# The order of three matmuls in each block of a split float32 product

## The chip, the core and the metric

The kernel runs on one core of one Trainium2 chip. The metric is the device time of one execution in microseconds; several executions are timed and the median is given. A profile is one more execution, recorded by the hardware profiler.

## The reference

Two layers of a decoder on one sequence of 256 tokens with 2048 channels, all in float32. Layer 0 mixes tokens by a convolution module, layer 1 by stick-breaking attention with 16 heads; each is followed by a gated feed-forward part with a causal convolution of width 3. Cut to what matters here:

```python
for i in range(DEPTH):                      # DEPTH = 2
    shift, scale, gate = ada_ln(c, mix_mod_w[i], mix_mod_b[i])
    h = rms_norm(x, mix_norm_g[i]) * (1.0 + scale) + shift
    if i % N_MIXERS == 0:
        y = conformer_conv_module(h, ...)   # products pw1 and pw2
    else:
        y = stick_breaking_mixer(h, sb_qkv_w[j], sb_o_w[j])   # products qkv and o
    x = x + gate * y
    shift, scale, gate = ada_ln(c, ffn_mod_w[i], ffn_mod_b[i])
    h = rms_norm(x, ffn_norm_g[i]) * (1.0 + scale) + shift
    x = x + gate * conv_ffn(h, ...)         # products up (2048 to 11264) and down (5632 to 2048)
return rms_norm(x, final_norm_g)
```

## The kernel before

Activations lie with channels on the 128 partitions and the 256 tokens along the row: x is 16 tiles of 128 x 256. A product takes weights in pieces of 128 x 1024, that is eight blocks of 128 x 128. A block is one output tile `nb` (128 output channels) times one input tile `kt`.

A product in three parts replaces a float32 matmul by three matmuls in the type float32r. Weights and activations are split into a high part, which is the value cast to float32r, and a low part, which is the rest. For the weights ScalarE (ACT) makes the high tile `wh` (line 244) and VectorE (DVE) the low tile `wl` (line 248); both are in rings of four buffers. For the activations there is a pair of tiles for each kt: `zh`/`zl` for pw2 (lines 378 and 379), `hh`/`hl` for up and qk, `gh`/`gl` for down, `oh`/`ol` for o. The high tile is made on ACT, the low one behind it on DVE, out of the value and the high tile. Of each block the products high times high, high times low and low times high are summed in PSUM: three matmuls, each with its own weight load, with the activation tile as the moving operand (256 columns, 258 in a product's entry). In the code `xh` and `xl` stand for the high and low activation tiles.

`gemm` walks through the blocks of a product in the order that `plan` has written. There a product starts with a head: the first few output tiles (8 in pw2, 4 elsewhere) are done side by side, kt by kt, so that each kt serves several blocks in a row; `STAGGER` puts the last few kts of a head aside. Behind the head one output tile follows the other, and each runs through all kts.

```python
    if first > 1:
        head, nbs = nbs[:first], nbs[first:]
        s = min(stagger, len(kts) // 2)
        seq += [(n, k) for k in kts[:len(kts) - s] for n in head]
        seq += [(n, k) for n in head for k in kts[len(kts) - s:]]
    return seq + [(n, k) for n in nbs for k in kts]
```

Products in order of time: pw1 (plain float32, line 664), pw2, up and down of layer 0 in two halves, qk and v of the attention in four groups of heads (v has its own three matmuls, lines 1131 to 1133), o, up and down of layer 1. Between the blocks of pw2 some matmuls of the modulation run (line 577), and on DVE reductions for later modulations (line 331).

The order of instructions on each engine comes from the tile scheduler, which works with the program's order, dependencies and priorities; from line `in_order(here)` a stretch ahead of pw2 is fixed. Weights come over SP's DMA queue in program order, modulation rows over SP's and POOL's.

Of the kernel before, what the change touches and what calls it, by code (L numbers as in the profile page):

```python
# [117 lines left out]
def hybrid_trunk(ctx: ExitStack, tc: tile.TileContext, cfg: Cfg, io: dict):  # L118
    nc = tc.nc
# [15 lines left out]
    def psum_acc():  # L135
        return acc.tile([P, 512], F32, name="ps")
# [44 lines left out]
    def advance(gens, k):  # L181
        for g in list(gens[:k]):
            if next(g, "end") == "end":
                gens.remove(g)
# [69 lines left out]
    def pieces(name):  # L254

        for i in range(-(-len(cfg.plans[name]) // PB)):
            at = look["at"]
            assert stream[at] == (name, i)
            look["at"] += 1
            while len(raws) < min(len(stream), at + 1 + look["load"]):  # L260
                load_next()
            while len(parts) < min(len(stream), at + 1 + look["split"]):
                split_next()
            yield parts[at]

    def set_rate(name):
        for stem, rate in RATES.items():
            if name.startswith(stem):
                pace["rate"], pace["credit"] = rate

    def gemm(name, xh, xl, done, after=None, width=None, halves=0, ready=None, quiet=0,
             banks=()):

        set_rate(name)
        left, ps, paired, banks = {}, {}, [], list(banks)
        todo = -(-len(cfg.plans[name]) // PB)
        for nb, _ in cfg.plans[name]:  # L280
            left[nb] = left.get(nb, 0) + 1
        for blocks, wh, wl in pieces(name):
            for b, (nb, kt) in enumerate(blocks):
                while ready and not ready(kt):
                    advance(side, pace["heads"])
                first = nb not in ps
                if first and len(ps) < halves:
                    first = not paired
                    bank = psum_acc() if first else paired.pop()
                    ps[nb] = bank[:, 0:T] if first else bank[:, T:2 * T]  # L290
                    if first:
                        paired.append(bank)
                elif first:
                    ps[nb] = (banks.pop(0) if banks else psum_acc)()[:, :width or T]
                o = ps[nb]
                left[nb] -= 1
                c = slice(b * P, (b + 1) * P)
                nc.tensor.matmul(o, wh[:, c], xh[kt], start=first, stop=False, skip_group_check=halves > 0)  # L298
                nc.tensor.matmul(o, wh[:, c], xl[kt], start=False, stop=False, skip_group_check=halves > 0)  # L299
                nc.tensor.matmul(o, wl[:, c], xh[kt], start=False, stop=left[nb] == 0, skip_group_check=halves > 0)  # L300
                if left[nb] == 0:
                    with tc.high_priority(offset=PRIORITY):
                        done(nb, ps[nb])
            todo -= 1
            if todo < quiet:
                pace["rate"] = 0.0
            (after or tick)()
# [124 lines left out]
    class Entry:  # L432
# [31 lines left out]
        def product(self, name, done, table=None):  # L464
            need(self.m, 0)
            self.shift()
            n, state = len(cfg.plans[name]), {"i": 0}

            def after():
                state["i"] += 1  # L470
                i = state["i"]
                if i >= max(1, min(2, n // PB - 1)) and self.rs is None:
                    self.rs = self.rms.rstd()
                    if table:
                        act_tables(table)
                if self.rs is not None:
                    free = KD if i * PB >= n else min(i * PB // FIRST, max(0, KD - STAGGER))
                    with tc.high_priority(offset=PRIORITY if i * PB >= n else 0):
                        for kt in range(len(self.h), free):
                            self.h[kt] = modulate_tile(self.m, kt, self.rs, pool=kt % 8 < 5)  # L480
                tick()

            def scaled(nb, ps):
                b = tmp.tile([P, 2], F32, name="bcol", bufs=4)
                t = t256()
                nc.vector.tensor_copy(b, ps[:, T:T + 2])
                nc.vector.tensor_tensor(t, ps[:, :T], self.rs, op=ALU.mult)
                nc.scalar.activation(t, t, AF.Identity, bias=b[:, 0:1])
                done(nb, t)

            gemm(name, [self.raw[k][0] for k in range(KD)], [self.raw[k][1] for k in range(KD)], scaled, after=after,
                 width=T + 2)
            return [self.h[k][0] for k in range(KD)], [self.h[k][1] for k in range(KD)]


    with ExitStack() as cv:
# [448 lines left out]

        act_tables("sqrt_and_others")
        gemm("pw2", [z[0] for z in zs], [z[1] for z in zs], pw2_done, halves=8)
        drain(fill)


    def ffn(i, entry, out):
        m = f"ffn{i}"
        NG = KF // 2 + 1
        with ExitStack() as fs:
# [40 lines left out]

            hh, hl = entry.product(f"up{i}0a", up_done, "silu_and_others")
            gemm(f"up{i}0b", hh, hl, up_done, banks=[psum_b, psum_a])
            gemm(f"up{i}1a", hh, hl, up_done)
            need(m, 2)
# [306 lines left out]
```

## Time and profile before

| | |
|---|---|
| time, median of 3 runs | 2307.48 us (2307.41 to 2308.37) |
| profiled execution: span from its first to its last instruction | 2304.7 us; the page gives no other time of it |
| TensorE (PE) busy | 2270.8 us, 99% |
| weight loads (PEld) busy | 2168.1 us, 94% |
| DVE, ACT, POOL busy | 1736.7, 1164.4, 334.6 us |
| mean granted clock of TensorE | 0.997 |
| matmuls in the profile | 17834 |
| L298, L299 and L300 on `hh`/`hl`, `gh`/`gl` | 3264 and 1408 blocks |

Matmuls overlap: one lasts some 280 ns, and the next starts after some 117 ns. Busy time therefore says that PE always had a matmul in hand, not how fast they followed each other. To see that, one takes a stretch of the trace in which PE is busy without a break and divides its length by the number of matmuls that started in it.

The stages used below, in microseconds from the start: pw2 from 285 to 408, up of layer 0 to 668, down's first half to 792, up's second half to 1027, down's second half to 1155, attention to 1455, o to 1548, layer 1's feed-forward part to the end.

### The profile page before, as it was taken

The numbers are of one execution on the slowest core, as the hardware profiler recorded it, in microseconds if no ns is written. First come the engines' busy times: TensorE is split into PE (matmuls) and PEld (weight loads), VectorE is DVE, ScalarE is ACT, GpSimd is POOL, SyncE is SP. The second block draws the span as 40 slices with busy tenths as digits, with TensorE's granted clock in tenths as the row PEclk, the third lists the DMA queues.
The fourth block names the chain that finished last, engine by engine and source line by source line (L and its number), as shares of the span: only waits on it lengthen the run. The fifth ranks groups of instructions, "written<-read, shape, count | busy, mean of one in ns | idle before, by whom it ended". The sixth has DMA issues, their size and how long they took to land.

```text
span 2304.7 us, 44243 instructions
## 1 busy us (share of the span) xinstructions
PE 2270.8 (99%) x17834; PEld 2168.1 (94%) x17834; DVE 1736.7 (75%) x2386; ACT 1164.4 (51%) x1776; POOL 334.6 (15%) x478
## 2 busy tenths in 40 slices
PE   7999999999999999999999999999999999999997
PEld 5888678999999999999999999999999999999997
DVE  7689968899998899999975555668666545666654
ACT  2056655755543355554465555657555434555443
POOL 4058713200000000002111000121000000000010
PEclk9999999999999999999999999999999999999999
DMA  9988799789999999999854555555555555555553
GB/s 397 417 328 306 272 368 355 272 320 356 358 347 384 363 345 361 355 350 345 304 189 159 165 173 167 172 190 179 190 187 189 187 188 186 190 189 187 190 185 110
DMA packets 139167, 603.56 MB, mean 262 GB/s; under 512 B 15441, under 2 KB 15569, under 8 KB 115153
## 3 DMA queue, kind: packets, MB, share of 16 engines
q1 hardware_dynamic: 120242, 464.42, 56.0%
q0 software_dynamic: 18720, 136.32, 15.8%
q8 instruction: 139, 2.28, 0.4%
q14 instruction: 66, 0.54, 0.1%
HBM read 598.58 MB, written 2.10 MB: 261 GB/s over the span
## 4 chain that ended last, share of the span: by engine, by line
PE 88%; DVE 5%; DMA 4%; ACT 1%; issue 1%; POOL 0%; DVEq 0%; SPq 0%; POOLq 0%; ACTq 0%
PE ps L298 25%; PE ps L299 25%; PE ps L300 25%; PE ps L664 5%; DMA mraw<-in_mt_mix 3%; DVE mraw L331 2%; DVE wl L248 1%; PE ps L1133 1%; PE ps L1131 1%; PE ps L1132 1%; DMA mraw<-in_mt_ffn 1%; PE ps L577 1%; PE auxa L577 1%; DVE hl L382 0%; PE auxb L1132 0%
## 5 line engine op out<-in xcount | busy, mean ns | idle before, releaser
L248 DVE TENSOR_TENSOR wl<-raw,wh 128x1024 fp32r<-128x1024 f32 x688 | 842.9, 1229 | 412.7 <-ACT wh L244 408.0
L244 ACT CAST wh<-raw 128x1024 fp32r<-128x1024 f32 x688 | 719.5, 1048 | 823.9 <-PE ps L299 642.1
L298 PE MATMUL ps<-hh,wh 128*128 128x256 f32 (+1 forms) x3264 | 915.8, 281 | 0.0
L299 PE MATMUL ps<-hl,wh 128*128 128x256 f32 (+1 forms) x3264 | 912.1, 279 | 0.0
L300 PE MATMUL ps<-hh,wl 128*128 128x256 f32 (+1 forms) x3264 | 908.3, 278 | 0.1
L299 PEld LDWEIGHTS ps<-hl,wh 128*128 128x128 f32 x3264 | 617.7, 189 | 0.3
L300 PEld LDWEIGHTS ps<-hh,wl 128*128 128x128 f32 x3264 | 612.8, 188 | 0.7 <-DVE wl L248 0.7
L298 PEld LDWEIGHTS ps<-hh,wh 128*128 128x128 f32 x3264 | 612.7, 188 | 0.3
L299 PE MATMUL ps<-gl,wh 128*128 128x256 f32 x1408 | 396.0, 281 | 0.0
L300 PE MATMUL ps<-gh,wl 128*128 128x256 f32 x1408 | 393.7, 280 | 2.1 <-DVE wl L248 2.1
L298 PE MATMUL ps<-gh,wh 128*128 128x256 f32 x1408 | 394.9, 280 | 0.0
L331 DVE CUSTOM_DVE_ANT_0 mraw<-mraw,csr 128x2048 f32<-128x2048 f32 x152 | 348.2, 2292 | 46.3 <-DMA mraw<-in_mt_mix 30.2
L300 PEld LDWEIGHTS ps<-gh,wl 128*128 128x128 f32 x1408 | 265.5, 189 | 2.3 <-DVE wl L248 2.3
L299 PEld LDWEIGHTS ps<-gl,wh 128*128 128x128 f32 x1408 | 266.5, 189 | 0.0
L298 PEld LDWEIGHTS ps<-gh,wh 128*128 128x128 f32 x1408 | 265.6, 189 | 0.0
L397 POOL TENSOR_TENSOR sumsq<-sumsq,t 128x256 f32<-128x256 f32 x56 | 66.2, 1183 | 879.8 <-ACT t L393 879.5
L664 PE MATMUL ps<-hh,raw 128*128 128x256 f32 x832 | 188.8, 382 | 0.0
L664 PEld LDWEIGHTS ps<-hh,raw 128*128 128x128 f32 x832 | 157.8, 191 | 28.3 <-issue 5.8
L967 DVE SCALAR_TENSOR_TENSOR t<-ps,par,t 128x254 f32<-128x254 f32 x328 | 157.3, 480 | 3.9
L704 DVE SCALAR_TENSOR_TENSOR auxb<-u,cpar,auxb 128x256 f32<-128x256 f32 x297 | 121.6, 483 | 4.5 <-ACT auxb L688 3.7
L839 POOL TENSOR_TENSOR y<-y,hl 128x256 f32<-128x256 f32 x143 | 104.4, 730 | 13.4 <-ACT hl L713 3.3
L964 ACT ACTIVATE t<-ps,par 128x256 f32<-128x256 f32 x164 | 91.9, 560 | 0.0
(247 smaller groups left out, 2270.5 us busy)
## 6 DMA issues: line engine op xcount, KB each, us to landing
raw<-in_w_down SPq DMA_DIRECT2D x176, 512.0 KB, 4.5
mraw<-in_mt_ffn POOLq DMA_DIRECT2D x64, 1024.0 KB, 8.3
raw<-in_w_pw SPq DMA_DIRECT2D x96, 512.0 KB, 8.0
mraw<-in_mt_mix POOLq DMA_DIRECT2D x48, 1024.0 KB, 8.2
raw<-in_w_up01b SPq DMA_DIRECT2D x84, 512.0 KB, 7.0
raw<-in_w_up11b SPq DMA_DIRECT2D x84, 512.0 KB, 3.5
raw<-in_w_up00b SPq DMA_DIRECT2D x80, 512.0 KB, 7.6
raw<-in_w_up10b SPq DMA_DIRECT2D x80, 512.0 KB, 3.5
```

The lines of the kernel that those rows point to most:

```text
L244: nc.scalar.copy(wh[:, :n], v[:, :n])
L248: nc.vector.tensor_tensor(wl[:, :n], v[:, :n], wh[:, :n].bitcast(F32), op=ALU.subtract)
L298: nc.tensor.matmul(o, wh[:, c], xh[kt], start=first, stop=False, skip_group_check=halves > 0)
L299: nc.tensor.matmul(o, wh[:, c], xl[kt], start=False, stop=False, skip_group_check=halves > 0)
L300: nc.tensor.matmul(o, wl[:, c], xh[kt], start=False, stop=left[nb] == 0, skip_group_check=halves > 0)
L331: nc.vector.tensor_tensor_reduce(out=v, in0=v, in1=csr, scale=1.0, scalar=0.0, op0=ALU.mult, op1=ALU.add, accum_out=macc[:, nb:nb + 1])
L397: engine.tensor_tensor(self.sum, self.sum, sq, op=ALU.add)
L664: nc.tensor.matmul(banks[j][:, nb // KD * T:(nb // KD + 1) * T], w[:, b * P:(b + 1) * P], hf[kt], start=first, stop=left[j] == 0, skip_gro ...
L704: nc.vector.scalar_tensor_tensor(conv_ps[j], us[j % UBUFS][:, k:k + T], tap(j, k), conv_ps[j], op0=ALU.mult, op1=ALU.add)
L839: nc.gpsimd.tensor_tensor(ys[c], ys[c], pr, op=ALU.add)
L964: nc.scalar.activation(y, ps[:, :T], AF.Identity, bias=pc(f"fdb{i}", nb, 1), scale=w(FW - 1))
L967: nc.vector.scalar_tensor_tensor(y[:, s:], ps[:, :T - s], w(k), y[:, s:], op0=ALU.mult, op1=ALU.add)
```

## The change

The first two matmuls of each block change places: the high weights multiply the low activations first, then the high ones. The flag that starts a sum in PSUM stays with the first.

```diff
-                nc.tensor.matmul(o, wh[:, c], xh[kt], start=first, stop=False, skip_group_check=halves > 0)
-                nc.tensor.matmul(o, wh[:, c], xl[kt], start=False, stop=False, skip_group_check=halves > 0)
+                nc.tensor.matmul(o, wh[:, c], xl[kt], start=first, stop=False, skip_group_check=halves > 0)
+                nc.tensor.matmul(o, wh[:, c], xh[kt], start=False, stop=False, skip_group_check=halves > 0)
                 nc.tensor.matmul(o, wl[:, c], xh[kt], start=False, stop=left[nb] == 0, skip_group_check=halves > 0)
```

Line 298 thus reads `xl` and line 299 `xh`. Two blocks on PE behind the head of the second half of up, layer 0, kt 1 and kt 2 of one output tile, before (the names are output, moving tile, weights; the numbers behind them are buffers):

```order
L298 MATMUL ps_5556<-hh1_3805,wh_5443 128x256
L299 MATMUL ps_5556<-hl1_3806,wh_5443 128x256
L300 MATMUL ps_5556<-hh1_3805,wl_5444 128x256
L298 MATMUL ps_5556<-hh2_3812,wh_5443 128x256
L299 MATMUL ps_5556<-hl2_3813,wh_5443 128x256
L300 MATMUL ps_5556<-hh2_3812,wl_5444 128x256
```

The same two blocks on PE after:

```order
L298 MATMUL ps_5556<-hl1_3806,wh_5443 128x256
L299 MATMUL ps_5556<-hh1_3805,wh_5443 128x256
L300 MATMUL ps_5556<-hh1_3805,wl_5444 128x256
L298 MATMUL ps_5556<-hl2_3813,wh_5443 128x256
L299 MATMUL ps_5556<-hh2_3812,wh_5443 128x256
L300 MATMUL ps_5556<-hh2_3812,wl_5444 128x256
```

The weights keep their order; the high activation tile is now read by two matmuls in a row, and the next kt's low tile follows on a high one. The first two blocks of pw2 on PE before, with the semaphores that each waits for (`Activation` is ACT):

```order
L298 MATMUL ps_2395<-zh0_2259,wh_2187 128x256 [waits Activation_49,Pool_49]
L299 MATMUL ps_2395<-zl0_2260,wh_2187 128x256 [waits DVE_49]
L300 MATMUL ps_2395<-zh0_2259,wl_2188 128x256
L298 MATMUL ps_2395<-zh0_2259,wh_2187 128x256
L299 MATMUL ps_2395<-zl0_2260,wh_2187 128x256
L300 MATMUL ps_2395<-zh0_2259,wl_2188 128x256
```

The first two blocks of pw2 on PE after:

```order
L298 MATMUL ps_2395<-zl0_2260,wh_2187 128x256 [waits DVE_49,Pool_49]
L299 MATMUL ps_2395<-zh0_2259,wh_2187 128x256 [waits Activation_49]
L300 MATMUL ps_2395<-zh0_2259,wl_2188 128x256
L298 MATMUL ps_2395<-zl0_2260,wh_2187 128x256
L299 MATMUL ps_2395<-zh0_2259,wh_2187 128x256
L300 MATMUL ps_2395<-zh0_2259,wl_2188 128x256
```

The wait for DVE has moved to the first matmul. On the other engines the scheduler moves some instructions in the stage of pw2 and nowhere else. On DVE, while the z tiles are made (`y` and `t` are steps on the way to `zh`; a minus is before, a plus after):

```order
 L923 TENSOR_TENSOR y_196<-y_196,dm 128x256
 L924 TENSOR_TENSOR t<-y_196,rstd 128x256
+L248 TENSOR_TENSOR wl<-raw,wh 128x1024
 L379 TENSOR_TENSOR zl_2328<-t,zh_2327 128x256
 L923 TENSOR_TENSOR y_197<-y_197,dm 128x256
 L924 TENSOR_TENSOR t<-y_197,rstd 128x256
-L248 TENSOR_TENSOR wl<-raw,wh 128x1024
 L379 TENSOR_TENSOR zl_2336<-t,zh_2335 128x256
```

The low part of a weight piece is made ahead of the low part of kt 7 instead of behind it; two later pieces move in the same way, and their casts on ACT too.

## Prediction

> **What bounds the kernel now.** I read the page first: the busy line, the chain that ended last, and the groups of the three matmuls that the change touches.
>
> ```profile
> span 2304.7 us, 44243 instructions
> ...
> PE 2270.8 (99%) x17834; PEld 2168.1 (94%) x17834; DVE 1736.7 (75%) x2386; ACT 1164.4 (51%) x1776; POOL 334.6 (15%) x478
> ...
> L298 PE MATMUL ps<-hh,wh 128*128 128x256 f32 (+1 forms) x3264 | 915.8, 281 | 0.0
> L299 PE MATMUL ps<-hl,wh 128*128 128x256 f32 (+1 forms) x3264 | 912.1, 279 | 0.0
> L300 PE MATMUL ps<-hh,wl 128*128 128x256 f32 (+1 forms) x3264 | 908.3, 278 | 0.1
> ```
>
> PE is busy for 99% of the span, and the three lines of a block wait for nothing. Their 280 ns is the length of one matmul, which overlaps the next; what counts is the step, the time from one start to the next. The second view is the list of waits on PE: its rows from 400 us to the end (the first three here), and from the stage of pw2 (the last).
>
> ```profile
> PE ps L300 <- DVE wl L248: 2.1, 1, 2.1
> PE auxb L300 <- DVE wl L248: 0.8, 2, 0.4
> PE auxb L402 <- ACT t L393: 0.7, 1, 0.7
> PE ps L298 <- ACT t L942: 1.6, 1, 1.6
> ```
>
> So behind 400 us PE loses 3.6 us to waits, and there is nothing else to win or lose there but the step itself. The third view therefore is PE in stretches of one kind: window, busy time, matmuls, clock, DMA. Rows 1 and 2 are the up products of layer 0 behind their heads, row 3 the o product behind its head, rows 4 and 6 the heads of the two down products of layer 0, row 5 the rest of the first of them, row 7 the rest of layer 1's second.
>
> ```profile
> 442.58:668.03 225.45, 225.45 (x1934) 1.00 0.92 347
> 792.22:1027.42 235.20, 235.20 (x2019) 1.00 0.93 352
> 1477.92:1547.92 70.00, 70.00 (x603) 1.00 0.57 188
> 668.03:693.57 25.54, 25.54 (x219) 1.00 0.96 369
> 693.57:792.22 98.65, 98.65 (x843) 1.00 0.99 380
> 1027.42:1052.92 25.50, 25.50 (x218) 1.00 0.93 354
> 2193.06:2291.20 98.14, 98.14 (x839) 1.00 0.44 146
> ```
>
> The two or three matmuls that began ahead of a window are counted with it; without them these are 644, 672, 200, 72, 280, 72 and 279 blocks of three. A block takes 225.45/644 = 350.1, 235.20/672 = 350.0 and 70.00/200 = 350.0 ns in the h and o products, 98.65/280 = 352.3 and 98.14/279 = 351.8 in the rest of down, and 25.54/72 = 354.7 and 25.50/72 = 354.2 in the heads of down. Shapes, clock (1.00) and number of matmuls are the same in all, and the step differs although PE is never idle: 116.7 to 118.2 ns. The DMA share doesn't order them (0.57 gives 350.0, as 0.92 does). What distinguishes a head is in the code: four blocks in a row have the same kt, so in three of four block boundaries the high tile that ended one block (L300) is read again by the next block's first matmul. The same rise shows inside one product, on the same tiles: 354.7 - 352.3 = 2.4 and 354.2 - 351.8 = 2.4 ns.
>
> The Trainium skill ("TensorE: Matmul & The Clock Gate", section "Back-to-back issue gap") gives a step of N/2.4 + 2.5 ns at full clock, 109.2 ns for 256 columns whatever the operands, and its section "Step-by-step: what each phase is for" says that loading the next weights takes nothing from the running matmul's reads. The rows differ: at clock 1.00 no stretch is under 116.7 ns, and equal shapes differ by 1.5 ns.
>
> **The change part by part.**
>
> *Moving tiles (all 5,248 blocks; 3264 + 1408 on the page, and 576 in smaller groups).* No matmul, weight load or byte is added. The order of the weights (wh, wh, wl) stays. The moving tiles went high, low, high, then the next kt's high; they now go low, high, high, then the next kt's low. Each block thus has a low-to-high step as before, a step in which the same high tile is read twice running, and a high-to-next-low step in place of the high-to-next-high. The nearest rows for a high tile read twice running are the heads. I take their 2.4 ns per block against the rest of the same product as its price. I apply it to blocks behind heads, since the heads have that repeat already: 644 + 672 in each layer's up products (2,632), 448 in the attention's qk products behind the first (28 output tiles of 16), 200 in o: 3,280 blocks. 3,280 x 2.4 = 7.9 us. It puts them at 352.5 ns. The 1,120 blocks of down behind the heads stand at 352.05 on average without a repeat; I take them to the same 352.5, not above it, as whatever makes them slow seems to be of the same kind: 1,120 x 0.45 = 0.5 us. PE is never idle in these stretches, so all of it lies on the path. Bounds: 0 from below, if the step doesn't care; from above all blocks at the heads' 354.5: 3,280 x 4.4 + 1,120 x 2.45 = 14.4 + 2.7 = 17.1 us. A gain is bounded under the rivals.
>
> *The first matmul now waits for the low tile.* The rows of the timeline at the start of pw2:
>
> ```profile
> 285.25 0.43 DVE L379 TENSOR_TENSOR zl<-t,zh 128x256 fp32r<-128x256 f32 x1
> 285.57 0.38 PE L298 MATMUL ps<-zh,wh 128*128 128x256 f32 x1
> 285.79 0.32 PE L299 MATMUL ps<-zl,wh 128*128 128x256 f32 x1
> ```
>
> zl ends at 285.68, and the matmul that reads it began 0.11 later. The first matmul would start at 285.79 instead of 285.57: 0.2 us, on the path. The built program has 24 first reads of a low tile with a wait for DVE. The others cost at most one step each, as one matmul less stands ahead of the wait: 23 x 0.12 = 2.8 us. I take 0. In the instructions of L299 one row only shows PE idle for a low tile:
>
> ```profile
>   DVE ol L1103: 0.2, 1
> ```
>
> and in pw2, where 16 of the 24 are, the tiles lie ready long before. Here is zl of kt 7, the wl and the zl behind it, and PE's first read of kt 7:
>
> ```profile
> 311.16 0.43 DVE L379 TENSOR_TENSOR zl<-t,zh 128x256 fp32r<-128x256 f32 x1 [0.96 <-ACT zh L378]
> ...
> 312.30 1.22 DVE L248 TENSOR_TENSOR wl<-raw,wh 128x1024 fp32r<-128x1024 f32 x1
> 313.43 0.42 DVE L379 TENSOR_TENSOR zl<-t,zh 128x256 fp32r<-128x256 f32 x1
> ...
> 315.84 0.39 PE L298 MATMUL ps<-zh,wh 128*128 128x256 f32 x1
> ```
>
> *What the scheduler moves in pw2.* On DVE three wl splits now stand ahead of a zl instead of behind it, on ACT their wh casts likewise. This zl comes later by 1.22 us, or more where that wl waits for PE to give back its buffer, with the next y and zl queued behind it; the 315.84 - 311.59 = 4.2 us of lead covers it and grows further on. If that cover were gone, each of three moves could cost up to 1.2 us. Behind them a few reductions of the modulation change places with wl splits. One is this long:
>
> ```profile
> L331 DVE CUSTOM_DVE_ANT_0 mraw<-mraw,csr 128x2048 f32<-128x2048 f32 x152 | 348.2, 2292 | 46.3 <-DMA mraw<-in_mt_mix 30.2
> ```
>
> A wl behind one comes 2.3 us later, a wl ahead of one as much earlier. PE's only wait in the stage that such moves could lengthen or take away is the 1.6 us for L942. I take 0, with both ends: 1.6 us less, 2.3 us more. SP's DMAs keep their order; three of POOL's loads pass a few sums of squares and stay far ahead of their use.
>
> **Sum.** 7.9 + 0.5 + 0.2 = 8.6 us. The span of 2304.7 becomes 2313.3. The page has no other time of that execution; the median of the runs, 2307.5, lies 2.8 us over the span. Forecast: 2307.5 + 8.6 = 2316.1 us.
>
> **The rivals.**
>
> *The step doesn't care.* The counts of steps by kind stay: one low to high, one high to low, one high to high per block. If a step's length depends on these kinds, or on neither, the time is 2307.5 + 0.2 = 2307.7 us. For it: the three lines' shares of the chain are close.
>
> ```profile
> by line: PE ps L298 25.3%; PE ps L299 25.2%; PE ps L300 24.8%; PE ps L664 5.0%; DMA mraw<-in_mt_mix 3.0%; DVE mraw L331 2.0%; DVE wl L248 1.1%; issue 1.0%; PE ps L1133 1.0%; PE ps L1131 1.0%; PE ps L1132 1.0%; DMA mraw<-in_mt_ffn 0.9%; PE p
> ```
>
> Against it: the heads, which have the same kinds too, and take longer. They also change the output tile with each block, so a part of the 2.4 ns may be that and not the repeat. Chance 0.31. The skill's rule above, a step set by the columns alone, comes to the same time.
>
> *All blocks at the heads' level.* The 17.1 us above: 2307.5 + 17.1 + 0.2 = 2324.8 us. For it: every block would have a repeat, a head has one in three of four. Against: down's rest, without repeats, shows that 352 ns has other causes, which needn't add. Chance 0.14.
>
> *Reading the same tile again is cheaper: faster.* In the chain L300's matmuls have 24.8% and L298's 25.3%: 0.5% of 2304.7 = 11.5 us lie between a third of the matmuls and another. If a repeat saves as much against today's high-to-next-high step, the time is 2307.5 - 11.5 = 2296 us. It decides from 4.6 us, or 1.0 ns in each of the 4,400 blocks behind heads. Against: the heads have such repeats and are the slowest. Chance 0.12.
>
> **How the numbers follow.** Forecast 0.43 (its own range 2312 to 2321), doesn't care 0.31, heads' level 0.14, cheaper 0.12. 0.2% (4.6 us) is about what a measurement tells from no change, so: faster 0.12, same 0.31, slower 0.57. The range from 2302 to 2326 takes in the first three with pw2's ends (1.6 less, 2.3 more) and leaves out most of the last and the top of the third.
>
> **What would show it.** In the same stretches of the changed kernel: the up and o products at 352.5 ns per block (a stretch of 644 blocks in 227.0 us instead of 225.45), down's rest about the same, the heads unchanged. If the up stretches stay at 350.0, the step doesn't care; if they pass 354, the heads' level holds; under 349, a repeat is cheap. A first matmul of pw2 that starts 0.2 us later shows the moved wait. I am wrong in another way if PE shows new waits for low tiles or wl between 285 and 408 us, or if the attention's own matmuls shift.

## The result, and the profile after

The changed kernel takes 2323.0 us (median of 3 runs, 2321.1 to 2325.3) against 2307.5: slower by 0.65% (ratio 1.0065, 95% interval 1.0051 to 1.0079). The forecast was 2316.1 in a range of 2302 to 2326.

From the page of the changed kernel, the span, the busy line and the groups of the three matmuls of h (instruction, count, busy us, mean ns, idle us ahead):

```profile
span 2319.3 us, 44248 instructions
...
PE 2283.1 (98%) x17834; PEld 2179.0 (94%) x17834; DVE 1736.3 (75%) x2386; ACT 1163.3 (50%) x1776; POOL 334.3 (14%) x478
```

```profile
L300 PE MATMUL ps<-hh,wl 128*128 128x256 f32 (+1 forms) x3264 | 919.1, 282 | 0.0
L299 PE MATMUL ps<-hh,wh 128*128 128x256 f32 (+1 forms) x3264 | 915.3, 280 | 0.0
L298 PE MATMUL ps<-hl,wh 128*128 128x256 f32 (+1 forms) x3264 | 914.6, 280 | 0.0
```

The span is 14.6 us longer, PE is about as full as before, and it still waits for nothing in these lines. The names up and down take two digits from here on, the layer and the half of the product: down01 is the second half of down in layer 0; up00b is up00 without its first four output tiles, up01b is up01 without its first two. The stretches of one kind, after (window, length, busy time and matmuls, clock, DMA share, GB/s): up of layer 0 in two parts, o behind its head, the two heads of down, the rest of down00, the rest of down11.

```profile
445.72:673.27 227.55, 227.55 (x1935) 1.00 0.92 345
797.69:1035.13 237.44, 237.44 (x2018) 1.00 0.92 349
1486.92:1557.58 70.66, 70.66 (x602) 1.00 0.55 186
673.27:698.76 25.49, 25.49 (x218) 1.00 0.94 359
1035.13:1060.65 25.52, 25.52 (x219) 1.00 0.90 346
698.76:797.69 98.93, 98.93 (x842) 1.00 0.99 381
2207.32:2305.81 98.49, 98.49 (x839) 1.00 0.43 145
```

A block of up takes 227.55/644 = 353.3 and 237.44/672 = 353.3 ns instead of 350.1 and 350.0; o 70.66/200 = 353.3 instead of 350.0; the heads of down 354.0 and 354.4 (354.7 and 354.2 before); the rest of down 353.3 and 353.0 (352.3 and 351.8). By the first matmul of each stage the 14.6 us are: the four up stages 8.6 (2.06, 2.24, 2.10, 2.24), the four down stages 1.5, attention 0.6, o 0.7, pw2 2.7 and its start 0.5.

Which of the three steps grew is read from the chain of the first up stretch by line, before and then after:

```profile
by line: PE ps L298 33.3%; PE ps L299 33.2%; PE ps L300 32.8%; PE auxa L300 0.2%; PE auxa L299 0.2%; PE auxb L298 0.1%; PE auxb L299 0.1%; PE auxa L298 0.1%; PE auxb L300 0.1%
```

```profile
by line: PE ps L300 33.4%; PE ps L299 33.1%; PE ps L298 32.8%; PE auxa L299 0.2%; PE auxa L300 0.2%; PE auxb L300 0.1%; PE auxb L299 0.1%; PE auxa L298 0.1%; PE auxb L298 0.1%
```

L300 goes from 0.328 x 225.45 = 73.9 to 0.334 x 227.55 = 76.0 us, L299 from 74.9 to 75.3, L298 from 75.1 to 74.6. By the starts of the matmuls in the settled blocks of this stretch, the step from L298 to L299 went from 117.6 to 116.7 ns; the one from L299 to L300, which now leads from the first read of the high tile to the second, from 117.0 to 117.9; and the one behind L300, which now leads to the next kt's low tile, from 115.4 to 118.7. So the step between the two reads of one tile grew by 0.9 ns and the one behind them by 3.3. That is a first hint that the repeat may not be what costs, and no proof: the second read may itself fill the step behind L300.

pw2's start on PE:

```profile
286.06 0.36 PE L298 MATMUL ps<-zl,wh 128*128 128x256 f32 x1 [0.18 <-DVE zl L379]
286.25 0.28 PE L299 MATMUL ps<-zh,wh 128*128 128x256 f32 x1
```

And PE's waits (us in total, times, longest), the first in down, the other two in pw2:

```profile
PE ps L300 <- DVE wl L248: 3.3, 3, 1.9
...
PE ps L298 <- ACT t L942: 2.5, 1, 2.5
...
PE ps L298 <- DVE zl L379: 0.2, 1, 0.2
```

The moved wait is there with 0.2 us. The longer wait for `t` (2.5 for 1.6 us) comes back below.

### The profile page after: what moved, and what is told of

It is laid out like the page before. It is cut to its first block, busy times and chain, and to the rows that moved or that the text cites. A ratio compares the mean times of both kernels' runs of the same rounds, so it can differ in the third digit from the quotient of the medians.

```text
span 2319.3 us, 44248 instructions
## 1 busy us (share of the span) xinstructions
PE 2283.1 (98%) x17834; PEld 2179.0 (94%) x17834; DVE 1736.3 (75%) x2386; ACT 1163.3 (50%) x1776; POOL 334.3 (14%) x478
## 4 chain that ended last, share of the span: by engine, by line
PE 86%; DVE 6%; DMA 5%; issue 1%; ACT 1%; POOL 0%; SPq 0%; DVEq 0%; POOLq 0%; ACTq 0%
PE ps L300 25%; PE ps L298 25%; PE ps L299 24%; PE ps L664 5%; DMA mraw<-in_mt_mix 3%; DVE mraw L331 2%; DMA mraw<-in_mt_ffn 2%; DVE wl L248 1%; PE ps L1131 1%; PE ps L1132 1%; PE ps L1133 1%; PE ps L577 1%; PE auxa L577 1%; DVE hl L382 0%; PE auxb L1132 0%
## 5 line engine op out<-in xcount | busy, mean ns | idle before, releaser
L300 PE MATMUL ps<-hh,wl 128*128 128x256 f32 (+1 forms) x3264 | 919.1, 282 | 0.0
L299 PE MATMUL ps<-hh,wh 128*128 128x256 f32 (+1 forms) x3264 | 915.3, 280 | 0.0
L298 PE MATMUL ps<-hl,wh 128*128 128x256 f32 (+1 forms) x3264 | 914.6, 280 | 0.0
L298 PEld LDWEIGHTS ps<-hl,wh 128*128 128x128 f32 x3264 | 616.7, 189 | 0.3
L299 PEld LDWEIGHTS ps<-hh,wh 128*128 128x128 f32 x3264 | 613.7, 188 | 0.3
L300 PEld LDWEIGHTS ps<-hh,wl 128*128 128x128 f32 x3264 | 613.1, 188 | 0.6 <-DVE wl L248 0.6
L300 PE MATMUL ps<-gh,wl 128*128 128x256 f32 x1408 | 396.0, 281 | 3.3 <-DVE wl L248 3.3
L299 PE MATMUL ps<-gh,wh 128*128 128x256 f32 x1408 | 394.6, 280 | 0.0
L298 PE MATMUL ps<-gl,wh 128*128 128x256 f32 x1408 | 393.8, 280 | 0.0
L300 PEld LDWEIGHTS ps<-gh,wl 128*128 128x128 f32 x1408 | 264.7, 188 | 3.9 <-DVE wl L248 3.9
L298 PEld LDWEIGHTS ps<-gl,wh 128*128 128x128 f32 x1408 | 265.8, 189 | 0.0
L299 PEld LDWEIGHTS ps<-gh,wh 128*128 128x128 f32 x1408 | 264.8, 188 | 0.0
```

What stands on the lines that cost most here:

```text
L298: nc.tensor.matmul(o, wh[:, c], xl[kt], start=first, stop=False, skip_group_check=halves > 0)
L299: nc.tensor.matmul(o, wh[:, c], xh[kt], start=False, stop=False, skip_group_check=halves > 0)
```

## The experiments

Theory 1 is the prediction's: a high tile read twice running costs 2.4 to 3.3 ns, wherever it lies. Theory 2: the tiles' places decide; what it says of them changes from run to run, as each text beforehand gives it. A tile's *phase* here is its start within a partition, in units of 32 bytes, modulo 256 bytes, from the addresses in the built program. In the kernel before, hh of kt 0, 1, 2, 3 lies at phases 1, 3, 5, 7 and so on in a ring, each hl one on, and every weight slice at phase 1. The change alters the sequence of phases that PE reads: h, h+1, h becomes h+1, h, h. Where times by phase or block are given without a row, they come from the starts of the matmuls in the trace.

### Other reads in the up stages

```diff
-                matmul(wh, xh[kt]); matmul(wh, xl[kt]); matmul(wl, xh[kt])
+                up00b: (wh, xh[kt]), (wh, xh[kt]), (wl, xh[kt])
+                up01b: (wh, wh, wl) on xh[(3 * kt + 0, 1, 2) % KD]
+                up10b: (wl, xh[kt]), (wh, xh[kt]), (wh, xl[kt])
+                up11b: (wl, xh[kt]), (wh, xl[kt]), (wh, xh[kt])
```

> The kernel before, with another set of three reads in one stage each: up00b reads the high tile three times (its low products are left out), up01b reads three high tiles that follow one another in the buffer, tiles 3kt, 3kt+1, 3kt+2 modulo 16 (its low products are left out too), up10b goes wl*high, wh*high, wh*low, and up11b goes wl*high, wh*low, wh*high. All four ran at 350.1 ns a block before, and at 353.3 after the change. Theory 1, that of the prediction (a tile read twice running costs 2.4 to 3.2 ns a block, wherever it lies): up00b, with two repeats, 355 to 356.5; up01b, with none, 350; up10b, with one, 352.5 to 353.3; up11b, with none, 350. Theory 2 (a matmul's step depends on which tile follows which: from one high tile to the next high tile is the cheap step, 115.4 ns, any other takes 117.4 to 118): up00b, two repeats and one cheap step, 350 to 351.5; up01b, three cheap steps, 346 to 347; up10b, whose last step goes from low to the next high, 353; up11b, which keeps the cheap step between blocks, 350. Theory 3 (only the order of the weights counts, or nothing but the low tile's place in the block): up00b and up01b 350.

The four stretches (of the second halves, the last 580 blocks; the last 32 blocks of the first and the third row belong to up01a and up11a, which have the old reads):

```profile
442.99:671.48 228.49, 228.49 (x1934) 1.00 0.91 345
828.33:1034.23 205.90, 205.90 (x1742) 1.00 0.93 351
1589.41:1817.37 227.96, 227.96 (x1935) 1.00 0.59 191
1973.76:2176.76 203.00, 203.00 (x1743) 1.00 0.59 189
```

228.49/644 = 354.8, 205.90/580 = 355.0, 227.96/644 = 354.0, 203.00/580 = 350.0 ns. Without the 32 blocks the first and third settle at 355.0 and 354.2. The first lies in theory 1's range and the third within 0.9 ns of it, but the second doesn't: without any repeat it is as slow as the first with two. It doesn't suit theory 2 in this form either, which gave it 346. The fourth shows that the order of the weights is not it: the same sequence of moving tiles as before, with another order of weights, takes the same 350.0.

### The change everywhere but in pw2

```diff
+                x1, x2 = (xh[kt], xl[kt]) if name == "pw2" else (xl[kt], xh[kt])
```

> The change everywhere but in pw2, which keeps high, low, high. pw2 took 122.20 us from its first matmul before and 124.89 after, with 3.05 us of it in one wait on t, and started 0.49 later. If the loss in pw2 comes from its own order (its first read of zl, and the moves of the side work there), pw2 is back at 122.2 and its start at 285.6, and the span is some 3 us under that after the change: 2316.3, with the stretches of up and down as after (227.5 and 98.9 us). If it comes from what the scheduler makes of the rest, pw2 stays at 124.9 and the span at 2319.3.

The stage of pw2 as a window, and PE's waits in it (in this kernel L300 is the first matmul of a block and L944 the line that was L942):

```profile
285.89:410.30 124.41, 120.39 (x952) 1.00 0.91 350
```

```profile
PE ps L300 <- ACT t L944: 4.0, 3, 2.1
```

The span was 2316.4, as expected, but not for the reason expected: pw2 kept 124.41 us, with 4.0 us of waits for `t`, although all five engines have the order of before there. So neither branch of the expectation holds. The 2.9 us under the changed kernel lie elsewhere: 2.3 in down01 (126.3 for 128.6 us), 0.6 ahead of up.

### The order of before, other places

`SKEW` is the padding behind each high and low tile of a product, in units of 32 bytes; g0 and g1 are the tiles of down in layer 0 and layer 1.

```diff
-SKEW = {"z": (1, 1), "g0": (1, 1), "g1": (1, 1), "o": (1, 1)}
+SKEW = {"z": (1, 1), "g0": (0, 0), "g1": (1, 2), "o": (2, 2)}
-        return [hpool.tile(..., name=f"{n}{i}") for n in ("hh", "hl")]
+        return [hpool.tile(..., name=f"{n}{i}") for n in ("hl", "hh")][::-1]
```

> The order of the kernel before; only where tiles lie is changed: each pair of h is allocated low tile first, g0 has no padding, g1 has other paddings (1 and 2 for 1 and 1), o has 2 and 2. Theory 1 (the repeat alone costs, places don't): the stretches behind the heads stay where they were, h at 350.1 ns a block, down at 352.3 and 351.8, o at 350.0. Theory 2 (which tile follows which, by its place): h, where the step from high to next high keeps its distance of two slots and the other two steps change sign, moves by under 1 ns; at least one of down00 (all distances multiples of 1024 bytes) and down01 moves by more than 1 ns from 352.3 and 351.8.

The two up stretches, and down00 behind its head:

```profile
444.33:671.89 227.56, 227.56 (x1934) 1.00 0.92 344
829.73:1034.66 204.93, 204.93 (x1742) 1.00 0.93 352
697.52:797.20 99.68, 99.68 (x842) 1.00 0.98 377
```

227.56/644 = 353.4 and 204.93/580 = 353.3: the whole loss of the change, with the order of before and no tile read twice running. Only hh and hl have changed places; every engine has the instructions of the kernel before in the same order. down00, every tile at phase 5, takes 99.68/280 = 356.0. The run took 2321.3 us (one run). Theory 1's forecast for it, 350.1, falls here; so does the part of theory 2 that said h would move by under 1 ns. That a repeat costs something besides is not yet excluded. pw2, with the order and the z tiles of before, took 123.92 us in this run.

### The changed order, the same places

The edit is that of the run above, made to the changed kernel.

> The changed order, low tile first in the block, with the tiles placed as in the run with the order of before and the new places. Theory 1: as after the change, h at 353.3 ns a block, down at 353.3 and 353.0, o at 353. Theory 2 by distance: in h the step from high to the next low is now two slots on and the pair's own step one slot on, so if the cheap step is one of distance it comes back, and h is at 350 to 351; if it is one of kind (any step on to a low tile is dear, from high to next high cheap) h stays at 353.3.

Up, then down00 behind its head:

```profile
444.80:673.42 228.62, 228.62 (x1934) 1.00 0.91 343
699.05:798.73 99.68, 99.68 (x842) 1.00 0.98 376
```

None of the three: 228.62/644 = 355.0. o reached 360.0 ns, and the run took 2328.2 us, the slowest of this study (one run). So it is no rule of distance or kind; it needed a map. One thing in it speaks already: down00, where every tile is at phase 5, takes the same 99.68 us with a repeat in every block as without one in the run above.

### A map of sequences

```diff
+                if name in MAPPED and nb in MAPPED[name]:
+                    low, e, f, p = PATTERNS[MAPPED[name][nb]]
+                    h = p + f * kt        # at(x): a tile of h at phase x mod 8
+                    three = [at(h + e), at(h), at(h)] if low else [at(h), at(h + e), at(h)]
```

> A map. In the four up stages behind their heads each of 160 output tiles has its own sequence of moving tiles (so the up outputs are wrong: products are of tiles picked by address alone); all else is the kernel before. A tile's phase is its start in units of 32 bytes modulo 256. Sequence high-first: phases p, p+e, p in a block and p+f in the next; sequence low-first: p+e, p, p, and p+f in the next; e from 0 to 7, f from 1 to 7, each output tile 16 blocks. The kernel before is high-first with e=1, f=2, the changed one low-first with e=1, f=2. Theory 2, now by phase: the time of a block is a function of the sequence of phases alone, so the map repeats what other runs measured where it holds their sequence: high-first e=1, f=2 at 350.0 ns, high-first e=7, f=2 at 353.3 (the run with the low tile placed first), low-first e=1, f=2 at 353.3, low-first e=7, f=2 at 355.0; and the other sequences spread over 8 ns or more, in both orders, with the means of the two orders within 1 ns of each other. Theory 1 (a repeat costs 2.4 to 3.3 ns): high-first sequences at 350 whatever e and f, but e=0 at 355 to 357; low-first at 353.3, but e=0 at 355 to 357.

The last 8 block steps within each output tile average 348.3 to 360.0 ns over the 160 sequences; high-first means 354.4, low-first 354.6. For f=2, p=1:

```
e            0      1      2      3      4      5      6      7
high-first 355.0  353.5  353.2  355.0  353.2  351.6  350.0  355.0
low-first  355.0  353.4  351.6  355.9  355.0  355.0  355.0  354.1
```

Order as such costs 0.2 ns on average, and e=0 isn't special. Of the four known values three came again: low-first e=1 with 353.4, and from p=2, as in the runs with the low tile placed first, high-first e=7 with 353.4 and low-first e=7 with 355.0. But before's own sequence (high-first, e=1) gave 353.5, not 350.0. In the kernel before, too, the first 14 blocks of the first up stretch are uneven (350 to 360 ns) and only then repeat 348, 353, 348, 351 to the end: a sequence has to settle, and one output tile can be too short for it. (up01's stretch, which follows on down00, repeats from its first block.)

### Held phases, and longer stretches

```diff
+PATTERNS = ([(0, e, 0, p) for p in range(8) for e in range(8) for _ in range(2)] +
+            [x for x in (<eight sequences>) for _ in range(4)])
```

> A second map (the up outputs are again wrong: tiles are picked by address alone). 128 of the 160 output tiles hold the phase from block to block (p, p+e, p, for all p and e from 0 to 7, two output tiles each, so 32 blocks): in such a sequence high-first and low-first are the same sequence, turned by one. The last 32 hold eight sequences of the first map for four output tiles each (64 blocks), to see where they settle: high-first e=1 f=2 (the kernel before's own), low-first e=1 f=2 (the changed one's), low-first e=1 f=6 from p=1 and from p=2, low-first e=3 f=6, high-first e=5 f=2, high-first e=6 f=7, low-first e=6 f=6. Theory 2 by phase, with settling: the first map gave 353.5 for the kernel before's own sequence in its one output tile, since a sequence needs some 16 blocks to settle (the kernel before's first 16 blocks behind its heads ran at 353.4 and all the rest at 350.0); over 64 blocks the first settles at 350.0 in its last 32 and the second at 353.3; and the held phases, all equal in what they read, differ by 4 ns or more among themselves. If the time of a block is instead set by chance at a stage's start, the two take other values than 350.0 and 353.3. Theory 1: held phases at 350, with e=0 at 355 to 357, the same for all p.

Rows for two output tiles each (32 blocks): held e=0 at p=1, p=2 and p=7, held e=3 at p=7, and the last 32 blocks of before's sequence, of the changed one and of low-first e=6 f=6:

```profile
535.28:546.80 11.52, 11.52 (x98) 1.00 0.96 358
626.26:637.46 11.20, 11.20 (x98) 1.00 0.99 381
1772.32:1783.23 10.91, 10.91 (x98) 1.00 0.61 193
1941.34:1952.85 11.51, 11.51 (x98) 1.00 0.52 184
2009.39:2020.59 11.20, 11.20 (x98) 1.00 0.55 188
2031.91:2043.22 11.31, 11.31 (x98) 1.00 0.52 188
2167.60:2178.74 11.14, 11.14 (x98) 1.00 0.59 190
```

Before's own sequence settles at 11.20/32 = 350.0 and the changed one at 11.31/32 = 353.4, next to each other in one stage. Low-first e=6 f=6 settles at 11.14/32 = 348.1 by the row and 348.3 by its block starts: with a repeat in every block it is faster than the kernel before. One of the eight sequences, low-first e=1 f=6 from p=1, has not settled in 64 blocks (353.6, 352.5, 354.1 and 353.4 by output tile). Among held phases, e=0 (the same phase in every read) goes from 360 (p=1) over 350 (p=2) to 340 (p=7; 10.91/32 is 341 with its first blocks, and 340.0 settled). All 64, in the second output tile, over the same 8 steps as in the first map:

```
p \ e   0      1      2      3      4      5      6      7
0     355.0  353.4  360.0  353.2  351.5  353.4  356.6  353.4
1     360.0  360.0  353.2  353.5  353.4  353.2  353.4  355.6
2     350.0  353.4  353.4  353.4  355.5  353.4  355.4  353.6
3     353.4  355.0  353.4  353.4  350.2  353.2  356.6  353.5
4     360.0  356.6  352.6  356.0  356.6  355.4  353.2  353.4
5     356.1  352.9  353.4  353.2  360.0  357.9  351.5  355.9
6     351.9  353.2  356.0  353.4  355.0  355.0  354.1  353.2
7     340.0  356.6  353.2  360.0  353.4  353.4  356.8  353.4
```

p=5, e=0 is what down00 had in the two runs with other places: 356.1 here, 356.0 there, in both orders. The map carries over to another product.

### z, g and o at phase 7, in the order of before

`SHIFT` is the size of a tile, in floats, that is put ahead of the first tile of a product.

```diff
+SKEW = {"z": (0, 0), "g0": (0, 0), "g1": (0, 0), "o": (0, 0)}
+SHIFT = {"z": 32, "g0": 16, "g1": 16, "o": 16}
+        if kind not in shifted:
+            shifted[kind] = pool.tile([P, SHIFT[kind]], F32, name="shift")
```

> The order of the kernel before. Only places are changed: the tiles of z, g and o have no padding (a stride of 1024 bytes) behind a shift of 128, 64 and 64 bytes, so that every one of them starts at phase 7, the sequence that the map of held phases showed at 340.0 ns a block (and other held phases at 350 to 360). Theory 2 by phase: down behind its heads at 340.0 for 352.3 and 351.8, its heads at 340 to 342 for 354.7 and 354.2, o at 340 for 350; pw2, which waits for other engines, within 1 us of before; up unchanged. By that: 4 x (280 x 12 + 72 x 14) ns = 17.5 us and 208 x 10 ns = 2.1 us less, about 2288. If the map's figure belongs to the up stages alone (other work beside it), down stays within 350 to 356 and the time is 2303 to 2313. Theory 1: unchanged, 2307.

Up, then down00 behind its head:

```profile
444.71:670.16 225.45, 225.45 (x1934) 1.00 0.90 336
694.66:789.86 95.20, 95.20 (x843) 1.00 1.00 396
```

95.20/280 = 340.0 ns, up unchanged, 2288.2 us: ratio 0.9915 (0.9899 to 0.9932), with PE's instructions in the order of the kernel before. Two stages did not follow: pw2 took 123.7 us for 122.2, outside the expected 1 us, and down01 gained 1.3 us instead of 4.4, as PE waits there for wl (3.7 us for 2.1).

### The changed order with places for it

```diff
+            for n, i in (("hl", 1), ("hh", 0), ("hl", 0), ("hh", 3), ("hl", 3), ("hh", 2), ("hl", 2), ("hh", 1)):
+                homes_h[n, k + i] = hpool.tile([P, T + 2], F32R, name=f"{n}{k + i}")
```

> The changed order (low, high, high), with z, g and o at phase 7 as in the run beside it, and the tiles of h in other slots: high tiles at phases 2, 0, 6, 4, the low tile one on, a sequence that the second map showed settling at 351.7 with low first. Theory 2 by phase: down and o as in the run beside it, within 0.5 ns a block, though low comes first (340); up behind its heads at 351.7 for 353.3; about 2288 + 2632 x 1.7 ns + 3 us in pw2 = 2295. Theory 1: the repeat still costs 2.4 to 3.3 ns in every block, 2320 or more.

```profile
445.88:672.37 226.49, 226.49 (x1935) 1.00 0.90 336
696.86:792.06 95.20, 95.20 (x843) 1.00 1.00 396
```

Up at 226.49/644 = 351.7, down00 at 340.0 with low first as with high first. 2298.7 us, ratio 0.9962 (0.9949 to 0.9975); 3.7 us over the expected 2295. By the stages of the two profiled runs it is 4.2 us longer in up than the run beside it, as expected, and 3.4 in pw2, its start and down01 together.

### A search among the sequences that h's 32 slots allow

```diff
+                    low, *phases = PATTERNS[MAPPED[name][nb]]
+                    vh, vl = at(phases[2 * (kt % 4)]), at(phases[2 * (kt % 4) + 1])
```

> A third map (up outputs wrong, tiles picked by address alone): 80 sequences, two output tiles each, in which all eight phases serve four neighbouring k tiles, as the 32 slots of h allow; picked from all such sequences by the mean steps of tile triples in the runs so far, which give them 349.3 to 351.2 ns a block. Theory 2 by phase: settled values from 345 to 356, some under the 350.0 of the kernel before. If steps depend on the pair of tiles alone and not on how the sequence settles, all lie within 1 ns of the 349.3 to 351.2.

A miss: the 80 settle between 350.0 and 358.4, three of them at 350.0 (before's own among them, and one with low first), none under it. Mean steps of three neighbouring tiles do not foretell where a sequence settles.

### h at phase 7 too, in both orders

```diff
-        return [hpool.tile([P, T + 2], F32R, name=f"{n}{i}") for n in ("hh", "hl")]
+        return [hpool.tile([P, T + 64], F32R, name=f"{n}{i}")[:, :T + 2] for n in ("hh", "hl")]
+SHIFT = {..., "h": 48}
+        shifted["end"] = hpool.tile([P, 16], F32, name="end")
-MORE_ROWS = 4
+MORE_ROWS = 3
-                home = row_homes[n] if near else ("zmm"[n % 3] ...) if "z" in cpar else "m"
+                home = row_homes[n] if near else "m"
```

> The order of the kernel before, all moving tiles of z, g, o and now h at phase 7 (each tile of h takes 1280 bytes for 1056; for the room one of the four row buffers of the convolution and the row buffer beside z are left out, so rows of the modulation arrive later in the first 410 us), the weights at phase 1 as before. Theory 2 by phase: up behind its heads at 340.0 for 350.1 and 350.0, 26 us less than with z, g and o alone at phase 7 (2288.2), some 2 us less in attention: 2260, and 0 to 15 us back in the convolution and pw2 for the buffers: 2260 to 2275. If h doesn't follow (another pool, other neighbours), 2288 to 2303.

> The run beside it with the changed order (low, high, high) everywhere but in pw2. All tiles start at one phase, so the sequence of phases is the same in both orders. Theory 2 by phase: up, down and o at 340.0 in both, the time within 1.5 us of the run beside it: the change costs nothing where the sequence of phases does not change. Theory 1 (a tile read twice running costs 2.4 to 3.3 ns a block): 3,280 blocks and 1,120 of down, 8 to 14 us more than the run beside it.

Up, down00 behind its head and o behind its head, high first:

```profile
441.91:660.87 218.96, 218.96 (x1934) 1.00 0.92 344
685.35:780.55 95.20, 95.20 (x842) 1.00 1.01 398
1456.89:1524.89 68.00, 68.00 (x602) 1.00 0.56 193
```

The same with low first:

```profile
443.68:662.64 218.96, 218.96 (x1934) 1.00 0.91 343
687.12:782.32 95.20, 95.20 (x842) 1.00 1.01 402
1456.31:1526.98 70.67, 70.67 (x603) 1.00 0.55 186
```

High first: 2259.9 us, ratio 0.9793 (0.9781 to 0.9806), the fastest version of this study; the missing row buffers cost nothing that shows ahead of up, which began at 406.6 us (407.8 before). down01 alone gained nothing, 129.8 us for 128.0, as PE waits 6.6 us there for wl. Low first: 2264.0 us; its ratio, 0.9848 (0.9806 to 0.9889), is that of six runs, two of which took 2287.8 and 2287.9.

Up and down00 are equal to 0.01 us, 218.96/644 = 340.0 and 95.20/280 = 340.0, although every block with low first reads its high tile twice running. Theory 1 is gone there. But the medians lie 4.1 us apart and not within 1.5, and o differs, 68.00 against 70.67 us for the same 200 blocks, with the same phases in both: 340.0 and 353.3 ns. The order is not what does it. With low first too, o ran at 340.0 in the kernel of "The changed order with places for it" (first row), and the high-first kernel itself stands at 353.3 for 30 blocks of the attention (second row):

```profile
1479.51:1547.50 67.99, 67.99 (x602) 1.00 0.55 192
1192.38:1202.98 10.60, 10.60 (x93) 1.00 0.49 167
```

So a sequence can settle at more than one value. In the kernels with z, g and o at one phase, every stretch of ten or more blocks at 353.3 begins behind a wait of PE or behind other matmuls, and so does every return to 340.0 within a product; why a restart takes the one value or the other is not shown. Whether this is what made the two long runs long is not known, as there is no trace of them: 25 us would be some 1,900 blocks at 353.3 instead of 340.0, an estimate from these rows.

### Is it the phase, or the phase beside the weights?

The edit is that of the high-first kernel above without a pad of 64 bytes behind h, which moves all that is allocated later.

> As the run with all tiles of h, z, g and o laid without rotation, in the order of before, but the weights now start at phase 7 instead of 1, h at 7, and z, g and o at 5. Two forms of theory 2. Relative: what counts is the phase of the moving tile less that of the weights that are loaded beside it (6 was the cheap one, from 7 less 1): down and o, at 5 less 7, that is 6, run at 340; up, at 7 less 7, that is 0, runs at the 360 that the second map showed for phase 1 with e=0. Absolute: the moving tile's own phase counts: up at 340, down and o at 355.8 to 356 (the map's phase 5 with e=0).

Up, down00 behind its head, o behind its head:

```profile
444.90:676.74 231.84, 231.84 (x1935) 1.00 0.89 328
701.24:796.44 95.20, 95.20 (x843) 1.00 1.00 399
1492.32:1560.32 68.00, 68.00 (x602) 1.00 0.56 193
```

Up, at phase 7 as before this edit, goes to 231.84/644 = 360.0; down00 and o, now at phase 5, stay at 340. The time is 2322.9 us (one run). Both numbers are those of the relative form, and 20 and 16 ns away from the absolute one. What counts is where the moving tile starts against something allocated behind h. The weights are what PE reads besides; the other buffers behind h moved as well, so that it is the weights is the likeliest reading and not shown by itself.

The Trainium skill ("TensorE: Matmul & The Clock Gate", section "Step-by-step: what each phase is for") says that loading the next weights takes no read bandwidth from the running matmul. Two kernels that differ in places only, at 340 and 360 ns a block, would speak against it if it is the weights that count, which no run here shows by itself. The Trainium skill's gap in the same page, section "Back-to-back issue gap", by its formula an estimate of 109.2 ns for 256 columns, was not reached: the best here is 340.0/3 = 113.3. The Trainium skill calls it there the gap of an isolated matmul, and says that in a stream the weight loads set the spacing too; the prediction took it for the step of a stream.

## Why the prediction was right and wrong

**The sign and the range were right, the reason was not, so the sign was luck.** The step that failed is "the nearest rows for a high tile read twice running are the heads. I take their 2.4 ns per block against the rest of the same product as its price". Heads and rest have different sequences of phases, as before and after have. No price of the repeat shows where places are held apart from it: with all phases equal up and down00 take 340.0 in both orders, with all at phase 5 down00 takes 356.0 in both, and without any repeat h takes 353.3 when its pairs are swapped. The change cost 3.3 ns a block because h+1, h, h settles at 353.3 where h, h+1, h settles at 350.0. With other places it could have gained: over the first map the two orders average 354.4 and 354.6, and one low-first sequence settles at 348.3. A caution stood in the prediction ("a part of the 2.4 ns may be that and not the repeat"), but among its rivals was none in which places matter.

**Terms.** h and o were put at 7.9 us; up, attention and o measured 8.6 + 0.6 + 0.7 = 9.9, so the size was 3.3 and not 2.4 in up. Down was put at 0.5; its stages grew by 1.5 (0.24, 0.63, 0.24 and 0.36 in order of time), since its rest stands at 353.3 and 353.0 and not at 352.5; in down01, the 0.63, PE's waits for wl also went from 2.1 to 3.3 us. The first matmul's wait was put at 0.2 and is 0.2; pw2 began another 0.3 later because zl itself came later. pw2's moves were put at 0, with ends -1.6 and +2.3; the stage grew by 2.7, above the end. Whether the moves did that stays open: with the order of before in pw2, and its tiles at the same phases, six other profiled runs had 122.0 to 124.7 us for the 122.2 of before, so the stage varies by 2 us and more for reasons that lie elsewhere.

**Rivals.** "The step doesn't care" (2307.7) fell. "All blocks at the heads' level" (2324.8) came nearest to the 2323.0, and by chance: the blocks stand at 353.3, not at 354.5. "Cheaper" read the cheap L300 step rightly and drew the wrong conclusion: the step behind L300 was cheap in the old sequence (115.4 ns) and is the dearest in the new one (118.7).

**What would show it.** Up stretches at 227.0 were named and 227.55 came; heads unchanged within 0.7 ns, as named. The wrong mechanism had all its own signs in the changed kernel's profile; only edits that separated place from order could tell.

## What to carry to other kernels

Where PE is never idle and equal matmuls still differ by a few ns, look at the tiles' start addresses before the order: here places alone moved a block between 340 and 360 ns. When a reorder of reads gains or loses a per cent, repeat it with the tiles placed otherwise before blaming the order. And take a price from a neighbouring stretch only if you can say what else differs between the two.

## What the runs showed of the hardware that was not expected

- The step of a 128 x 256 matmul at clock 1.00 with PE never idle lay between 340/3 = 113.3 and 360/3 = 120.0 ns by where the moving tiles start modulo 256 bytes. Values that a long stretch of h settles at repeat to 0.1 ns across stages or runs (350.0, 351.7, 352.5, 353.3, 355.0).
- Most sequences settle within some 16 blocks and then repeat themselves (seven of eight that were run for 64 blocks). Where one settles was not foretold by the mean steps of its parts. The same phases can stand at 340.0 or 353.3, in either order of the reads; which of them changed only at a wait or at other matmuls.
- One phase for all moving tiles, 6 units (192 bytes) beyond that of the weights modulo 256 bytes, was the fastest of all that were tried: 2.1% of the kernel's time, with the matmuls of its products in the same order and only their addresses changed.
